# Rotary scores over 128 rows with each head's rotary k standing twice, in a float32 hybrid encoder trunk

## The chip, the cores and the metric

The kernel runs on one core of one Trainium2 chip. Its engines, as the profile names them: PE (TensorE, matmuls) with PEld (its weight loads), DVE (VectorE), ACT (ScalarE), POOL (GpSimd) and SP (SyncE), whose queue issues nearly all DMAs. The metric is the device time of one execution in microseconds, as a median over runs.

## The reference

A trunk of two layers on 512 positions and 2048 channels, in float32. The first layer is a gated pooling mixer; from its output come one shared key and value side, and then a layer of latent attention with 16 heads:

```python
def qk_norm_rope(t, g, cos, sin):
    t = rmsnorm(t, g)
    return jnp.concatenate([t[..., :QK_NOPE], apply_rope(t[..., QK_NOPE:], cos, sin)], axis=-1)
...
def pool_mixer_layer(x, norm_g, w_in, w_group, scale, w_out):
    h = rmsnorm(x, norm_g)
    proj = h @ w_in
    u, gate = proj[..., :W_A], proj[..., W_A:]
    u = u.reshape(B, S, N_POOL_GROUPS, G_A)
    pooled = jnp.stack(
        [causal_mean_pool(u[:, :, gi], w) - u[:, :, gi] for gi, w in enumerate(POOL_WINDOWS)],
        axis=2)
    y = jnp.einsum('bsgc,gcd->bsgd', pooled, w_group).reshape(B, S, W_A) * scale
    y = y * jax.nn.silu(gate)
    return x + y @ w_out
...
    for i in range(S // QBLOCK):
        q0, k_end = i * QBLOCK, (i + 1) * QBLOCK
        s = jnp.einsum('bqhd,bkhd->bhqk', q[:, q0:k_end], k[:, :k_end],
                       preferred_element_type=jnp.float32) * scale
        s = jnp.where(mask[None, None], s, -1e30)
        p = jax.nn.softmax(s, axis=-1).astype(v.dtype)
        outs.append(jnp.einsum('bhqk,bkhd->bqhd', p, v[:, :k_end]))
```

The pool windows are 2, 4, 8 and 16, one for each group of channels. The mask is causal by chunks of 64 positions. Each head's q and k have 128 plain channels (`QK_NOPE`) and 64 rotary ones (`QK_ROPE`), so a score is a sum over 192 products. The rotary k is the same for all heads up to the norm, which is taken per head.

## The kernel before

Products of float32 are made of three matmuls: each operand is split into a high part (a cast to fp32r, on ScalarE) and a low part (the rest, a subtraction on VectorE); high by high, low by high and high by low are added in PSUM. `split` (L144, L145) does it for activations and `load_w` (L120 to L122) for weights, which are loaded through the SP queue into `raw`.

**Stages, with their times in the profiled execution.** The pool mixer's input product runs to 698.6 us, within `with ExitStack() as c1`, where it has tile pools of its own (`xcp`, `epool`, `w7`, `ps7`); its results go to DRAM tiles (`scr`, L337). Then come the grouped products (`pooled_tile` and `y_tile`, weights `awg`) and the mixer's output product (`awo`) to about 1240. `pooled_tile` loads a 128x512 piece of the mixer's input from DRAM (L391) into a tile of `tpool` and pools and splits it; `y_tile` loads the gate (L400) and multiplies by `awg`. Eight pieces of group 0 are made ahead of the first product. `tpool` has six buffers of 512 columns (tag "t", tiles called `tt_`) and is opened once, for the whole kernel. Latent products and gates follow to about 1530, attention to 1835, and the output product (`bwo`) to the end.

**Attention** goes by head pairs, `hg` from 0 to 7. What a pair needs is prepared by `prep_units`: the kv product in four pieces (`kv_unit`, k0 to k3 in the planner's list, L570 to L572), the q product in four (`q_unit`, q0 to q3, L590 to L592, its result copied from PSUM by ScalarE, L595), the norms, and six transposes of 128x512 (`tr_unit`, L655): T0 and T1 turn the plain k of the two heads, T2 the rotary k of both heads at once (head 0 in rows 0 to 63, head 1 in rows 64 to 127), T3 and T4 the plain q and T5 the rotary q, again of both heads. `attn_units` has for each head four score units of 128 queries by 128, 256, 384 and 512 keys (`score_unit`, L696), each followed by the softmax (memset of the masked corner L697, reduction L699, its scaling L701, exponential L704 on ScalarE, reciprocal L705, scaling L706), the transposes of its probabilities (`pt_unit`, L715) and, after every second, the product with the values (`pv_unit`, L740 to L742).

The order in which the units are written comes from a hand-made list (`PREP`) and two constants that say when a piece of the next pair's preparation comes due among the units of this pair's attention. From there on the order on each engine is set by a scheduler in the tile framework: each engine then runs its own list strictly in order, and waits on semaphores for the others. A wait is for a whole tile, not for the rows of it that are used, and an engine that reads a PSUM tile is ordered behind another engine that reads it. PSUM tiles: three `mm` (products), two `sc` (scores), two `tr` (transposes), one `ov`.

**Rotary parts before.** T2 leaves one tile `kh` with the high parts of both heads (one cast of 128x512, L659) and per head a tile that has its low part in its own 64 rows (L660, L661) and a copy of its high part in the other 64 (L662, L663). T5 leaves per head a tile with the high part of q in the head's own 64 rows (L668, L669) and the low part in the others (L670, L671). A score unit is five matmuls: three of the plain parts over 128 rows, then high by high over the head's 64 rows, then one over 128 rows which adds high q by low k and low q by high k.

Of the kernel before, what the change touches and what calls it, by code (L numbers as in the profile page):

```python
# [14 lines left out]
P = 128  # L15
S = 512
# [35 lines left out]
def trunk_kernel(  # L52
# [21 lines left out]
    spool = ctx.enter_context(tc.tile_pool(name="spool", bufs=4))  # L74
    tpool = ctx.enter_context(tc.tile_pool(name="tpool", bufs=6))
    dpool = ctx.enter_context(tc.tile_pool(name="dpool", bufs=16, space=bass.MemoryType.DRAM))

    def xt(shape=(P, S), dt=F32):
        return xpool.tile(list(shape), dt, tag="x", name="xt")
# [7 lines left out]
    def tt_(n=S, dt=F32):  # L87
        return tpool.tile([P, n], dt, tag="t", name="tt_")

# [9 lines left out]
    def f(ap):  # L99
        return ap.bitcast(F32)  # L100
# [154 lines left out]

    with ExitStack() as c1:
        xcp = c1.enter_context(tc.tile_pool(name="xcp", bufs=NJ))
        epool = c1.enter_context(tc.tile_pool(name="epool", bufs=2))
# [123 lines left out]
    bpool = ctx.enter_context(tc.tile_pool(name="bpool", bufs=32, **tile_))  # L382
    xpool = ctx.enter_context(tc.tile_pool(name="xpool", bufs=16, **tile_))
    ps = ctx.enter_context(tc.tile_pool(name="ps", bufs=2, space=bass.MemoryType.PSUM, **tile_))

# [39 lines left out]


    xkv, xb, spill = [], [], []
    accs = [tt_(), tt_()]
# [80 lines left out]
    for t in range(4):  # L509
        junk = spool.tile([P, 192], F32, tag="junk", name="junk", bufs=2)  # L510
        A.activation(junk[:, 0:64], kr[:, t, :], AF.Square, accum_out=kr2[:, t:t + 1])
# [51 lines left out]
    def kv_unit(hg, t):  # L563
# [12 lines left out]
        for h in range(2):  # L576
            junk = spool.tile([P, 192], F32, tag="junk", name="junk", bufs=2)
            A.activation(junk[:, 0:128], d["kraw"][a][:, b, h * P:(h + 1) * P], AF.Square,
                         accum_out=d["ssk"][:, 2 * t + h:2 * t + h + 1])

    def q_unit(hg, t):
# [14 lines left out]
        for h in range(2):  # L596
            junk = spool.tile([P, 192], F32, tag="junk", name="junk", bufs=2)
            A.activation(junk, q[:, h, :], AF.Square, accum_out=d["ssq"][:, 2 * t + h:2 * t + h + 1])
# [43 lines left out]
    def tr_unit(hg, u):  # L642
# [13 lines left out]
        if u == 2:  # L656

            kh, k0, k1 = xt(dt=F32R), bt(), bt()
            A.copy(kh, p)  # L659
            V.tensor_tensor(k0[0:64, :], p[0:64, :], f(kh[0:64, :]), ALU.subtract)  # L660
            V.tensor_tensor(k1[64:128, :], p[64:128, :], f(kh[64:128, :]), ALU.subtract)  # L661
            V.tensor_copy(k0[64:128, :], f(kh[0:64, :]))  # L662
            V.tensor_copy(k1[0:64, :], f(kh[64:128, :]))  # L663
            d["kr"] = (kh, k0, k1)
            return
        if u == 5:
            q0, q1 = bt(), bt()
            A.copy(q0[0:64, :], p[0:64, :])  # L668
            A.copy(q1[64:128, :], p[64:128, :])  # L669
            V.tensor_tensor(q0[64:128, :], p[0:64, :], f(q0[0:64, :]), ALU.subtract)  # L670
            V.tensor_tensor(q1[0:64, :], p[64:128, :], f(q1[64:128, :]), ALU.subtract)  # L671
            d["qr"] = (q0, q1)
            return
# [9 lines left out]
    def score_unit(hg, h, i):  # L683
# [220 lines left out]
```

## Time and profile before

| | us |
|---|---|
| median of 3 runs | 1993.39 |
| lowest and highest | 1992.2, 1994.09 |
| the profiled execution | 1993.23 |
| its span in the trace | 1991.4 |
| its stages: pool mixer input | 0 to 698.6 |
| grouped and output products | to about 1240 |
| latent products, gates | to about 1530 |
| attention | to about 1835 |
| output product | to 1991.4 |

A row of the profile has the line of the kernel, the engine, the operation, what it writes and reads by the program's names, the shapes and the count; then the busy time in us and the mean of one in ns; then the idle time of the engine just before, with what ended it. In timelines a row starts with the start and the duration in us, and a bracket at its end is idle time before it. PE overlaps consecutive matmuls, so the time that one takes of the engine is read from the distance of starts. The granted clock of PE is given as a share of full speed.

### The profile page before, as it was taken

How to read it: one execution, taken by the hardware profiler on the slowest of the kernel's cores; microseconds unless marked ns; L12 is line 12 of the kernel's file. 1: busy time of each engine (PE TensorE's matmuls, PEld its weight loads, DVE VectorE, ACT ScalarE, POOL GpSimd, SP SyncE). 2: the span in 40 equal slices, each digit the busy share in tenths (PEclk: the TensorE clock that was granted, in tenths of full speed). 3: DMA queues.
4: the chain of work that ended last, by engine and by line, in shares of the span. 5: the costliest groups of instructions: out<-in, count | busy, mean ns of one | idle time of the engine just before them, and what ended most of it. 6: DMA issues, size and time to landing. Idle time of an engine off the chain costs nothing.

```text
span 1991.4 us, 30647 instructions
## 1 busy us (share of the span) xinstructions
PE 1941.2 (97%) x11372; PEld 1717.5 (86%) x11372; DVE 1289.7 (65%) x2291; ACT 815.8 (41%) x1527; POOL 299.1 (15%) x434
## 2 busy tenths in 40 slices
PE   5699999999999999999999999999999999999999
PEld 5699999999999978888888888888888788878887
DVE  6778866666666589377496567473344878787422
ACT  5433333333333353233333354233244767675221
POOL 2733432222222200000000000000010211110000
PEclk9799999999999999999999999999999999999999
DMA  4534544444444374344344344323332111121632
GB/s 157 175 111 134 168 129 138 128 135 125 135 127 134 121 243 159 106 127 148 112 128 136 107 144 132 94 92 99 96 94 76 51 42 46 50 65 48 211 121 87
DMA packets 167110, 235.53 MB, mean 118 GB/s; under 512 B 14640, under 2 KB 93360, under 8 KB 166960
## 3 DMA queue, kind: packets, MB, share of 16 engines
q1 hardware_dynamic: 166672, 233.37, 37.6%
q8 instruction: 89, 1.46, 0.3%
q14 instruction: 61, 0.50, 0.1%
q10 hardware_dynamic: 288, 0.20, 0.0%
HBM read 208.35 MB, written 25.17 MB: 117 GB/s over the span
## 4 chain that ended last, share of the span: by engine, by line
PE 93%; DVE 3%; DMA 1%; ACT 1%; issue 1%; POOL 0%; SPq 0%; DVEq 0%; ACTq 0%; POOLq 0%
PE mm L141 16%; PE mm L139 16%; PE mm L140 16%; PE k L320 10%; PE k L316 10%; PE k L318 10%; PE sc L696 3%; PE mm L570 1%; PE mm L571 1%; PE mm L572 1%; DMA raw<-awin 1%; PE tr L655 1%; PE mm L592 1%; PE mm L590 1%; PE mm L591 1%; PE tr L715 1%
## 5 line engine op out<-in xcount | busy, mean ns | idle before, releaser
L316 PE MATMUL k<-xh,hi 128*128 128x256 f32 x1792 | 493.7, 287 | 31.3 <-ACT hi L299 31.1
L318 PE MATMUL k<-xl,hi 128*128 128x256 f32 x1792 | 495.7, 286 | 0.9 <-DVE xl L284 0.8
L121 ACT CAST whi<-raw 128x512 fp32r<-128x512 f32 (+2 forms) x421 | 256.1, 611 | 537.0 <-PE mm L140 461.6
L320 PE MATMUL k<-xh,lo 128*128 128x256 f32 x1792 | 450.3, 287 | 4.9 <-DVE lo L300 4.9
L122 DVE TENSOR_TENSOR wlo<-raw,whi 128x512 fp32r<-128x512 f32 (+2 forms) x421 | 282.1, 672 | 225.6 <-ACT whi L121 221.8
L299 ACT CAST hi<-raw 128x1792 fp32r<-128x1792 f32 x128 | 216.2, 1690 | 406.9 <-PE k L320 260.5
L300 DVE TENSOR_TENSOR lo<-raw,hi 128x1792 fp32r<-128x1792 f32 x128 | 266.2, 2080 | 179.2 <-ACT hi L299 179.2
L316 PEld LDWEIGHTS k<-xh,hi 128*128 128x128 f32 x1792 | 348.0, 195 | 32.3 <-ACT hi L299 31.9
L318 PEld LDWEIGHTS k<-xl,hi 128*128 128x128 f32 x1792 | 349.5, 195 | 1.3 <-DVE xl L284 1.3
L141 PE MATMUL mm<-bt,wlo 128*128 128x512 f32 x860 | 335.5, 390 | 0.0
L139 PE MATMUL mm<-bt,whi 128*128 128x512 f32 x860 | 334.7, 389 | 0.0
L140 PE MATMUL mm<-bt,whi 128*128 128x512 f32 x860 | 334.5, 389 | 0.0
L320 PEld LDWEIGHTS k<-xh,lo 128*128 128x128 f32 x1792 | 321.6, 195 | 6.9 <-DVE lo L300 6.4
L139 PE MATMUL mm<-at,whi 128*128 128x512 f32 x516 | 202.1, 393 | 2.6 <-ACT whi L121 2.5
L141 PE MATMUL mm<-at,wlo 128*128 128x512 f32 x516 | 202.3, 392 | 1.7 <-DVE wlo L122 1.7
L140 PE MATMUL mm<-at,whi 128*128 128x512 f32 x516 | 202.3, 392 | 0.0
L141 PEld LDWEIGHTS mm<-bt,wlo 128*128 128x128 f32 x860 | 161.5, 188 | 34.2 <-issue 0.5
L139 PEld LDWEIGHTS mm<-bt,whi 128*128 128x128 f32 x860 | 161.5, 188 | 33.7 <-issue 0.2
L140 PEld LDWEIGHTS mm<-bt,whi 128*128 128x128 f32 x860 | 161.5, 188 | 33.5
L295 POOL TENSOR_TENSOR raw<-raw 128x256 f32<-128x256 f32 x128 | 107.0, 836 | 421.8 <-DVE raw L293 408.1
L141 PEld LDWEIGHTS mm<-at,wlo 128*128 128x128 f32 x516 | 97.4, 189 | 23.8 <-DVE wlo L122 3.6
L139 PEld LDWEIGHTS mm<-at,whi 128*128 128x128 f32 x516 | 97.5, 189 | 23.0 <-ACT whi L121 3.0
(1148 smaller groups left out, 2434.3 us busy)
## 6 DMA issues: line engine op xcount, KB each, us to landing
raw<-awin SPq DMA_DIRECT2D x256, 256.0 KB, 3.3
raw<-awo SPq DMA_DIRECT2D x128, 256.0 KB, 2.7
raw<-bwin SPq DMA_DIRECT2D x80, 256.0 KB, 2.8
raw<-awg SPq DMA_DIRECT2D x64, 256.0 KB, 2.9
raw<-bwo SPq DMA_DIRECT2D x59, 256.0 KB, 2.8
scr<-e SPq DMA_DIRECT2D x56, 256.0 KB, 2.6
raw<-wkvb SPq DMA_DIRECT2D x32, 256.0 KB, 3.1
raw<-wqb SPq DMA_DIRECT2D x32, 192.0 KB, 2.4
```

The source lines that it names most:

```text
L121: A.copy(hi[:, :n], raw[:, :n])
L122: V.tensor_tensor(lo[:, :n], raw[:, :n], f(hi[:, :n]), ALU.subtract)
L139: T.matmul(dst, wh, xh, start=first, stop=False)
L140: T.matmul(dst, wh, xl, start=False, stop=False)
L141: T.matmul(dst, wl, xh, start=False, stop=last)
L295: G.tensor_tensor(c[:, :, 6, :], c[:, :, 4, :], c[:, :, 2, :], ALU.add)
L299: A.copy(hi, c[:, :, 1:8, :])
L300: V.tensor_tensor(lo, c[:, :, 1:8, :], f(hi), ALU.subtract)
L316: T.matmul(dst, hi[:, j % 2, wi, :], xh[j][:, xi, :], start=first, stop=False, skip_group_check=True)
L318: T.matmul(dst, hi[:, j % 2, wi, :], xl[j][:, xi, :], start=False, stop=False, skip_group_check=True)
L320: T.matmul(dst, lo[:, j % 2, wi, :], xh[j][:, xi, :], start=False, stop=last, skip_group_check=True)
L696: T.matmul(s[:, 0:n], l, r, start=(j == 0), stop=(j == 4))
```

## The change

**Scores.** The fourth matmul goes over 128 rows instead of 64. For that a head's rotary k stands twice: `krh` has its high part in rows 0 to 63 and again in 64 to 127, `krl` likewise its low part. The rotary q tile has high over low, for both heads now in the same rows (high in 0 to 63). The fourth matmul adds high q by high k and low q by high k, the fifth high q by low k and also low q by low k, a product that was not made before.

**The tiles from T2 and T5.** Of T2, per head and half, there is a cast and then a subtraction, eight steps where there were five; the two halves of a head are in the same tiles. Of T5 the same four steps are written in another order: cast, subtraction, cast, subtraction.

**Pools.** Head 0's `krh` is a tile of `rpool`. `junk`, a scratch output of ScalarE's sums of squares, has one buffer instead of two. `tpool` becomes three pools in turn: one that lives during the pool mixer's input product, one (opened behind `xpool`) for the grouped and output products, one for the rest. The second's six tiles take addresses that `w7`, the weight tiles of the pool mixer, had; before, `tpool` overlapped nothing.

```diff
--- before.py
+++ after.py
...
-    tpool = ctx.enter_context(tc.tile_pool(name="tpool", bufs=6))
+    ca = ExitStack()
+    tp = [None]
...
     def tt_(n=S, dt=F32):
-        return tpool.tile([P, n], dt, tag="t", name="tt_")
+        return tp[0].tile([P, n], dt, tag="t", name="tt_")
...
     with ExitStack() as c1:
+        tp[0] = c1.enter_context(tc.tile_pool(name="tpool1", bufs=6))
         xcp = c1.enter_context(tc.tile_pool(name="xcp", bufs=NJ))
...
     xpool = ctx.enter_context(tc.tile_pool(name="xpool", bufs=16, **tile_))
+    tp[0] = ca.enter_context(tc.tile_pool(name="tpool2", bufs=6, **tile_))
...
+    ca.close()
+    tp[0] = ctx.enter_context(tc.tile_pool(name="tpool3", bufs=6, **tile_))
     xkv, xb, spill = [], [], []
...
-        junk = spool.tile([P, 192], F32, tag="junk", name="junk", bufs=2)
+        junk = spool.tile([P, 192], F32, tag="junk", name="junk", bufs=1)
...
         if u == 2:
 
-            kh, k0, k1 = xt(dt=F32R), bt(), bt()
-            A.copy(kh, p)
-            V.tensor_tensor(k0[0:64, :], p[0:64, :], f(kh[0:64, :]), ALU.subtract)
-            V.tensor_tensor(k1[64:128, :], p[64:128, :], f(kh[64:128, :]), ALU.subtract)
-            V.tensor_copy(k0[64:128, :], f(kh[0:64, :]))
-            V.tensor_copy(k1[0:64, :], f(kh[64:128, :]))
-            d["kr"] = (kh, k0, k1)
+
+            d["kr"] = []
+            for h in range(2):
+                src = p[h * 64:h * 64 + 64, :]
+                kh, kl = (xt(dt=F32R) if h else rpool.tile([P, S], F32R, tag="r", name="kr0")), bt()
+                for o in (0, 64):
+                    A.copy(kh[o:o + 64, :], src)
+                    V.tensor_tensor(kl[o:o + 64, :], src, f(kh[o:o + 64, :]), ALU.subtract)
+                d["kr"].append((kh, kl))
             return
         if u == 5:
             q0, q1 = bt(), bt()
-            A.copy(q0[0:64, :], p[0:64, :])
-            A.copy(q1[64:128, :], p[64:128, :])
-            V.tensor_tensor(q0[64:128, :], p[0:64, :], f(q0[0:64, :]), ALU.subtract)
-            V.tensor_tensor(q1[0:64, :], p[64:128, :], f(q1[64:128, :]), ALU.subtract)
+            for h, q in enumerate((q0, q1)):
+                src = p[h * 64:h * 64 + 64, :]
+                A.copy(q[0:64, :], src)
+                V.tensor_tensor(q[64:128, :], src, f(q[0:64, :]), ALU.subtract)
             d["qr"] = (q0, q1)
...
-        krh, krx = d["kr"][0], d["kr"][1 + h]
+        krh, krl = d["kr"][h]
         qh, ql_ = d[("T", 3 + h)]
         qr = d["qr"][h]
         qs = slice(i * P, (i + 1) * P)
-        hs = slice(h * 64, h * 64 + 64)
         ops = [(qh[:, qs], kh[:, 0:n]), (qh[:, qs], kl[:, 0:n]), (ql_[:, qs], kh[:, 0:n]),
-               (qr[hs, qs], krh[hs, 0:n]), (qr[:, qs], krx[:, 0:n])]
+               (qr[:, qs], krh[:, 0:n]), (qr[:, qs], krl[:, 0:n])]
```

How this moves instructions is seen in the order on three engines. Lines of the kernel after are a few higher (L655 becomes L660, L696 L702, L715 L721, L391 L394, L595 L600, L704 L710). First TensorE around the rotary and plain q transposes of a steady head pair, before: the transposes of T5 (`tt__15837` is the rotary q), two score units of this pair's second head, T3 between them, the transposed probabilities of an earlier unit, T4, and the first score unit of the next pair.

```order
L655 MATMUL tr<-cs,tt__15837 128x128 x4
L696 MATMUL sc<-bt 128x384 x3
L696 MATMUL sc<-xt,bt 128x384
L696 MATMUL sc<-bt 128x384
L655 MATMUL tr<-cs,xt 128x128 x4
L696 MATMUL sc<-bt 128x512 x3
L696 MATMUL sc<-xt,bt 128x512
L696 MATMUL sc<-bt 128x512
L715 MATMUL tr<-cs,tt__16006 128x128 x4
L655 MATMUL tr<-cs,xt 128x128 x4
L696 MATMUL sc<-bt 128x128 x3
L696 MATMUL sc<-xt,bt 128x128
```

The same place after (`tt__15857` is the rotary q):

```order
L660 MATMUL tr<-cs,tt__15857 128x128 x4
L702 MATMUL sc<-bt 128x512
L702 MATMUL sc<-xt,bt 128x512
L702 MATMUL sc<-bt 128x512
L660 MATMUL tr<-cs,xt 128x128 x4
L702 MATMUL sc<-bt 128x128 x2
L721 MATMUL tr<-cs,tt__16030 128x128 x4
L702 MATMUL sc<-bt 128x256 x2
L660 MATMUL tr<-cs,xt 128x128 x4
L702 MATMUL sc<-bt 128x128
L702 MATMUL sc<-kr_15964,bt 128x128
L702 MATMUL sc<-bt 128x128
```

T5 stood ahead of the unit of 384 columns and now stands within the one of 512; T3, which stood ahead of that one, is now behind it, directly ahead of the next pair's first scores; and the next pair's units of 128 and 256 are begun in turn, two matmuls each, with T4 in between.

ScalarE around the rotary k, before: the cast of T2 (L659), then the two copies of the q product, a weight cast and an exponential.

```order
L121 CAST whi<-raw 128x512
L144 CAST xt<-tr 128x128
L659 CAST xt<-tr 128x512
L595 COPY xt<-mm 128x384 x2
L121 CAST whi<-raw 128x512
L704 ACTIVATE tt__15934,sm<-sc,nm,qy 128x384
L598 ACTIVATE junk,ssq<-xt 128x192 x2
```

The same place after, one pair on (`kr_16534` is head 0's high part, the casts on `xt` at L669 are head 1's):

```order
L710 ACTIVATE tt__16524,sm<-sc,nm,qy 128x384
L669 CAST kr_16534<-tr 64x512
L145 CAST xt<-tr 128x2x128
L710 ACTIVATE tt__16600,sm<-sc,nm,qy 128x512
L669 CAST kr_16534<-tr 64x512
L669 CAST xt<-tr 64x512
L600 COPY xt<-mm 128x384 x2
L710 ACTIVATE tt__16661,sm<-sc,nm,qy 128x128
L145 CAST bt<-tr 128x512
L710 ACTIVATE tt__16732,sm<-sc,nm,qy 128x256
L603 ACTIVATE junk,ssq<-xt 128x192
L669 CAST xt<-tr 64x512
```

The four casts are spread over this stretch, with the copies of the q product behind the third and the fourth eleven rows behind the first.

SP's queue at the end of the pool mixer's input product, before: its last stores to DRAM, three loads of `awg` and the seventh and eighth loads of pooled input (the first six, `tt__7476` to `tt__7506`, stand much earlier, among the loads of the mixer's last weights):

```order
L290 DMA raw<-awin 128x2x256 x6
L337 DMA scr<-e 256x1x256
L337 DMA scr<-e 128x512
L120 DMA raw<-awg 128x512 x3
L417 DMA xt<-xT 128x512
L391 DMA tt__7512<-scr 128x512
L417 DMA xt<-xT 128x512
L391 DMA tt__7518<-scr 128x512
```

And after, where the first load of pooled input (`tt__7480`) is the one that waits for the last matmul on the weight tiles that lay there:

```order
L339 DMA scr<-e 256x1x256
L339 DMA scr<-e 128x512
L394 DMA tt__7480<-scr 128x512
L394 DMA tt__7486<-scr 128x512
L394 DMA tt__7492<-scr 128x512
L394 DMA tt__7498<-scr 128x512
L394 DMA tt__7504<-scr 128x512
L394 DMA tt__7510<-scr 128x512
L121 DMA raw<-awg 128x512
L339 DMA scr<-e 256x1x256
L339 DMA scr<-e 128x512
L394 DMA tt__7516<-scr 128x512
```

All six first loads of pooled input now stand here, ahead of the first load of `awg`.

More of the change, by code (lines that the diff above doesn't have):

```diff
@@ L576, in kv_unit @@
         for h in range(2):
-            junk = spool.tile([P, 192], F32, tag="junk", name="junk", bufs=2)
+            junk = spool.tile([P, 192], F32, tag="junk", name="junk", bufs=1)
             A.activation(junk[:, 0:128], d["kraw"][a][:, b, h * P:(h + 1) * P], AF.Square,
@@ L596, in q_unit @@
         for h in range(2):
-            junk = spool.tile([P, 192], F32, tag="junk", name="junk", bufs=2)
+            junk = spool.tile([P, 192], F32, tag="junk", name="junk", bufs=1)
             A.activation(junk, q[:, h, :], AF.Square, accum_out=d["ssq"][:, 2 * t + h:2 * t + h + 1])
```

## Prediction

> **What bounds the kernel now.** I read the page first, then the windows of the attention stage, then the waits of TensorE there. The page's shares of busy time, and the first line of its chain:
>
> ```profile
> PE 1941.2 (97%) x11372; PEld 1717.5 (86%) x11372; DVE 1289.7 (65%) x2291; ACT 815.8 (41%) x1527; POOL 299.1 (15%) x434
> ...
> PE 93%; DVE 3%; DMA 1%; ACT 1%; issue 1%; POOL 0%; SPq 0%; DVEq 0%; ACTq 0%; POOLq 0%
> ```
>
> TensorE is busy 97% of the span and 93% of the chain, so matmul time taken away is time gained, unless something else then ends last. The change touches attention, so what counts is the limit there. Two windows, columns busy us of PE, PEld, DVE, ACT, POOL, then granted clock; the first is one steady head pair, the second the last pair, whose attention has no preparation beside it:
>
> ```profile
> 1584.31:1623.45 39.14, 38.51 (x218) 32.37 (x217) 31.99 (x114) 27.55 (x96) 6.61 (x16) 1.00 0.16 48
> ...
> 1779.90:1835.00 55.10, 54.17 (x280) 42.86 (x281) 42.56 (x139) 32.29 (x88) 3.66 (x9) 1.00 0.18 54
> ```
>
> A head pair takes 39.14 us and TensorE idles 0.63 of it. VectorE is busy 31.99, 82%: the second limit is near. TensorE's waits over five such pairs (total, times, longest):
>
> ```profile
> PE tr L715 <- DVE bt L671: 1.8, 5, 0.4
> PE tr L655 <- DVE bt L678: 1.3, 5, 0.3
> ```
>
> 3.1 us over five pairs, 0.62 each, both at the transposes around the q tiles. All the rest of VectorE's and ScalarE's work is hidden now.
>
> **The matmuls.** What the 64-row matmul costs is read from starts, since matmuls overlap. TensorE and its weight loads in two adjacent score units (384 and 512 columns), with the matmuls of 384 and 512 columns that ran back to back nearby:
>
> ```profile
> 1622.24 0.33 PE L590 MATMUL mm<-whi,at 128*128 128x384 f32 x1
> ...
> 1623.11 0.34 PE L592 MATMUL mm<-wlo,at 128*128 128x384 f32 x1
> 1623.29 0.68 PE L696 MATMUL sc<-bt 128*128 128x384 f32 x3
> 1623.89 0.44 PE L696 MATMUL sc<-xt,bt 64*128 64x384 f32 x1
> 1624.26 1.14 PE L696 MATMUL sc<-bt 128*128 128x384 f32 x4
> 1625.33 0.50 PE L696 MATMUL sc<-xt,bt 64*128 64x512 f32 x1
> 1625.76 0.51 PE L696 MATMUL sc<-bt 128*128 128x512 f32 x1
> 1626.11 0.27 PE L715 MATMUL tr<-cs,tt__15866 128*128 128x128 f32 x1
> ```
>
> ```profile
> 1623.89 0.18 PEld L696 LDWEIGHTS sc<-xt,bt 64*128 64x128 f32 x1 [0.25 <-issue]
> 1624.26 0.71 PEld L696 LDWEIGHTS sc<-bt 128*128 128x128 f32 x4 [0.18 <-issue]
> 1625.33 0.18 PEld L696 LDWEIGHTS sc<-xt,bt 64*128 64x128 f32 x1 [0.36 <-issue]
> ```
>
> ```profile
> 1629.42 0.40 PE L572 MATMUL mm<-wlo,at 128*128 128x512 f32 x1
> ...
> 1630.58 0.39 PE L571 MATMUL mm<-whi,at 128*128 128x512 f32 x1
> ```
>
> From 1622.24 to 1623.11 five matmuls of 384 columns start, 0.174 us apart; from 1629.42 to 1630.58 five of 512, 0.232 apart. Ten score matmuls at that pace take 5×0.174 + 5×0.232 = 2.03 us. They take 1626.11 − 1623.29 = 2.82, so 0.79 too long, 0.39 per unit. The loads show where: the weight load into 64 rows, and the 128-row one behind it, are not begun ahead under the running matmul but wait 0.18 to 0.36 us, with nothing to wait for by the profile. All 64 units have one such matmul (16 of each width):
>
> ```profile
> L696 PE MATMUL sc<-xt,bt 64*128 64x512 f32 x16 | 8.0, 499 | 0.0
> ```
>
> The new matmul is 128-row, with as many columns: an ordinary fifth of the unit. The gain on TensorE is 64 × 0.39 = 25.0 us, 8 × 0.39 = 3.1 per pair; I bound it by 22 and 27 (0.35 and 0.42 a unit), since the two narrower widths are taken to be like these.
>
> The Trainium skill, TensorEngine Tiling (Array Packing), section Overview, Theoretical Speedup, says that a contraction of at most 64 rows can go up to twice as fast with the array split, which speaks against this change: at half of a mean 0.145 us, giving up 64 such matmuls would cost about 5 us (an estimate by that page). The rows disagree (0.43 us from the start at 1625.33 to the next, where 128 rows take 0.232); its Key Properties say that a change of tiling mode drains TensorE, which the held loads fit.
>
> **The new tiles.** Durations of the pieces, from the groups by form and from the timelines of VectorE and ScalarE in one such pair (start, duration):
>
> ```profile
> L595 ACT COPY xt<-mm 128x384 f32<-128x384 f32 x32 | 14.3, 480 | 3.9 <-PE mm L592 3.9
> ...
> L678 DVE SCALAR_TENSOR_TENSOR bt<-tr,gqk,bt 128x512 fp32r<-128x512 f32 x15 | 10.8, 722 | 3.3 <-ACT bt L677 3.0
> ...
> L677 ACT ACTIVATE bt<-tr,gqk 128x512 fp32r<-128x512 f32 x15 | 10.3, 688 | 8.0 <-PE tr L655 8.0
> ...
> L671 DVE TENSOR_TENSOR bt<-tr,bt 64x512 fp32r<-64x512 f32 x8 | 5.5, 694 | 0.1
> ...
> L668 ACT CAST bt<-tr 64x512 fp32r<-64x512 f32 x8 | 4.6, 580 | 2.9 <-PE tr L655 2.8
> ```
>
> ```profile
> 1605.83 0.37 ACT L144 CAST xt<-tr 128x256 fp32r<-128x256 f32 x1
> 1606.10 0.79 ACT L704 ACTIVATE tt__15712<-sc,nm,qy 128x512 f32<-128x512 f32 x1
> ```
>
> ```profile
> 1604.47 0.67 DVE L699 TENSOR_REDUCE nm<-sc 128x1 f32<-128x512 f32 x1
> ...
> 1605.38 0.42 DVE L145 TENSOR_TENSOR xt<-tr,xt 128x256 fp32r<-128x256 f32 x1
> ...
> 1605.87 0.11 DVE L697 MEMSET sc<- 64x64 f32 x1
> ...
> 1606.50 0.28 DVE L699 TENSOR_REDUCE nm<-sc 128x1 f32<-128x128 f32 x1
> ...
> 1607.10 0.15 DVE L705 RECIPROCAL sm<-sm 128x1 f32<-128x1 f32 x1
> ...
> 1607.57 0.48 DVE L706 TENSOR_SCALAR tt__15712<-tt__15712,sm 128x512 f32<-128x512 f32 x1
> ```
>
> Busy time grows little: four 64-row casts for one cast (ScalarE +2.3 us a pair at most, 4 × 0.58), and two more subtractions in place of two copies (VectorE +1.4 at most, 2 × 0.69). VectorE's 31.99 + 1.4 = 33.4 would still fit a period of 39.1 − 3.1 = 36.0. What matters is order: in the built program each of the eight steps of the k tile waits for the one before it, across engines, and of the q tile the second cast now waits for the first subtraction. What stands behind a waiting cast on ScalarE waits as well. I walk both places with these durations and no time for handoffs.
>
> K tile, from the end of its transposes (0). ScalarE: cast 0.58, cast of the transposed probabilities 0.95, exponential of 512 columns 1.74 (its sum 0.09 later, an estimate), second k cast 2.41. VectorE: subtraction 1.27, memset 1.38, subtraction of the probabilities 1.80, reciprocal behind the exponential 1.98, reduction 2.26, scaling 2.74, second k subtraction 3.43. ScalarE: third k cast 4.01, and only then the copy of the q projection, 4.49, which frees the PSUM buffer of the next kv product. TensorE's own work is put at 0.058 us for 128 columns (a quarter of 0.232) and 0.09 for a transpose (an estimate: nearer to that than to the 0.27 of one alone). It has 0.67 us to do, then waits for the probabilities' cast until 0.95 (0.28), works to 1.07, waits for the exponential to free a score buffer until 1.74 (0.67), works 1.36 to 3.10, and waits for that buffer until 4.49 (1.39). Sum 2.3 us.
>
> Q tiles, from the end of the 512-column unit into which the rotary q transposes now fall (0). VectorE: memset 0.11, first q subtraction 0.80, reduction 1.47, 1.62, second q subtraction 2.31. ScalarE: second cast, behind the first subtraction, 1.38, and behind it the scaled cast of the next transposes, 2.07. TensorE has only those transposes (0.36), then waits until 2.07 for the next pair's first scores: 1.71. The rest follows alike: 0.1 each before two transposes and before the value products, then 1.4 before a transpose whose buffer VectorE frees behind two reductions (0.28 and some 0.4) and another scaled subtraction (0.72). Sum 3.4 us.
>
> Together 5.7 a pair, of which 0.6 is there already: 5.1 new against 3.1 gained. Five steady pairs: 25.5. The pair whose preparation comes first and is laid out differently: half, 2.6. For the last pair's 55 us the window shows VectorE free for 12.5 us, so its gain stays. Bounds of these waits: 5 us in all (the next engine is early nearly everywhere, as now) and 38 (a third more, since handoffs were left out). I take 28, near the walk's end, because it follows the program's own waits.
>
> **The pools.** The tiles of pooled input move to a place that overlaps the pool mixer's weight tiles, and so the first of their loads now waits for the last matmul of that stage; five more, and then the first weights of the next stage, stand behind it in SP's queue. Now three of those weight loads are issued before the last matmul. TensorE at the first matmuls of the next stage, the rate of all DMAs from 698 to 722 us in 40 slices with the time from issue to landing of a first one, and the window behind (granted clock third from the end):
>
> ```profile
> 701.16 0.80 PE L139 MATMUL mm<-at,whi 128*128 128x512 f32 x1 [2.54 <-ACT whi L121]
> ...
> 703.14 0.80 PE L141 MATMUL mm<-at,wlo 128*128 128x512 f32 x1 [0.76 <-DVE wlo L122]
> ```
>
> ```profile
> GB/s 0 0 0 0 0 20 259 389 379 239 236 311 379 270 232 273 338 314 376 396 403 396 403 413 403 410 393 393 382 399 382 386 389 389 382 382 386 389 386 386
> ...
> tt__7512<-scr SPq DMA_DIRECT2D x1, 256.0 KB, 2.7
> ```
>
> ```profile
> 701.10:707.90 6.80, 5.98 (x14) 4.30 (x15) 6.80 (x13) 3.74 (x8) 0.00 (x0) 0.53 0.88 278
> ```
>
> TensorE ends the pool mixer at 701.16 − 2.54 = 698.6. The first load, issued then, lands 2.7 later; the six others follow 0.67 us apart (256 KB at the 390 GB/s of the full queue), so the weights land at 705.3, and with a cast of 0.6 (the 0.58 above) the first matmul starts at 705.9, for 701.16: +4.8, less some of the 0.76, which data that lie there by then can spare. I take +4.5, with bounds of 2 (all of that and part of the later work's slack) and 7 (another stall of 2 on weights that queue behind). Half clock is paid now and would be paid then.
>
> The other edit, one junk buffer for two, costs nothing: all its writes are ScalarE's own, in order.
>
> **The sum.** −25.0 + 28 + 4.5 = +7.5. The profiled execution took 1993.23, span 1991.4, against a median of 1993.39 (1992.2 to 1994.09), so the two agree: 1993.4 + 7.5 = 2001. By the bounds of the waits alone it is 1993.4 − 25.0 + 4.5 + 5 = 1978 to 2011.
>
> **Rivals.** *The gain stays.* If the chains overlap with later slack, the pair falls by most of its 3.1 us. For it: VectorE idles 7 us a pair. Against it: TensorE's place in the queue is fixed, and slack elsewhere doesn't feed a wait here. With 5 us of waits 1978, with half of the walked 28, 1987; it decides below 20.5 us of waits, 3.7 a pair. *They cancel*, at waits of 16.5 to 24.5: 1989.4 to 1997.4, within 4 us of no change. *The clock drops.* The idle of 2.54 us at the handover is followed by a granted clock of 0.53 over 6.8 us. If waits of 1.4 to 1.7 did the same, two a pair would cost 2 × 6.8 × 0.47 = 6.4 us each of six pairs, 38 in all: 2039. Against it, this wait of 1.06 and the clock after it:
>
> ```profile
> 1544.97 0.79 PE L696 MATMUL sc<-xt 128*128 128x384 f32 x3 [1.06 <-ACT tt__14734 L704]
> ```
>
> ```profile
> 1543.80:1550.60 6.80, 5.74 (x26) 4.03 (x26) 5.17 (x15) 6.12 (x18) 1.53 (x5) 1.00 0.33 89
> ```
>
> The Trainium skill, TensorE: Matmul & The Clock Gate, section What's actually happening, puts half clock behind an idle window of about 3.4 us, longer than any wait here; by it this rival falls, though the 2.54 above was shorter and did bring 0.53. *The change does not do what it says*: the held loads come from changing operands and stay; then nothing offsets the 32.5, and it ends at 2026.
>
> **Chances.** Waits about as walked 0.44 (1998 to 2010); cancel 0.16; gain stays, half or nearly whole, 0.34; clock 0.03; held loads stay 0.03. 0.2%, 4 us, is what a measurement of this kernel can tell from none. Faster 0.34, same 0.16, slower 0.50. The range runs from 1975 to 2013: the 1978 and 2011 of the waits, each moved by about half of what the bounds of the other two terms add (27 and 2 instead of 25.0 and 4.5 one way, 22 and 7 the other). The likeliest case alone has 1998 to 2010.
>
> **What would show it.** Right: score units of about 1.2 us at 512 columns and no held loads; TensorE waiting 1 us and more for the q projection's copy and for the scaled cast, in each pair, at clock 1.00; a pair of 41 us; a first matmul of the second stage at 706. Wrong: a pair below 38 us, these waits under half a microsecond, or VectorE above 95% of a pair, which would make it a bound that the walk left out.

## The result, and the profile after

The change takes 2016.34 us (median of 4 runs, 2015.03 to 2017.9) against 1993.03 before: a ratio of 1.0117, 95% interval 1.0099 to 1.0134. Slower was forecast, but the 23 us lie outside the range, which ended at 2013. The page of after, as that of before was shown:

```profile
span 2016.1 us, 30664 instructions
...
PE 1933.3 (96%) x11372; PEld 1718.0 (85%) x11372; DVE 1309.6 (65%) x2291; ACT 829.6 (41%) x1551; POOL 297.7 (15%) x434
...
PE 85%; DVE 6%; ACT 4%; DMA 3%; issue 1%; POOL 0%; SPq 0%; DVEq 0%; ACTq 0%; POOLq 0%
```

TensorE is busy 8 us less, in a span 25 us longer: of the chain that ended last it held 93% and holds 85%, and VectorE, ScalarE and DMAs got the rest. So time went into waits. To see where, I set the n-th matmul of after against the n-th of before (both have 11372):

| from | to | before | after | more |
|---|---|---|---|---|
| first matmul | last of the pool mixer's input product | 683.0 | 683.3 | +0.3 |
| there | matmul 5600 (some 220 on) | 57.3 | 70.7 | +13.4 |
| there | first transpose of T2 | 717.4 | 717.2 | -0.1 |
| there (attention) | 500 matmuls from the end | 401.1 | 413.1 | +12.0 |
| there | last matmul | 113.1 | 113.1 | 0.0 |

The sum is 25.6, and the first matmul is 0.9 earlier. Two places, then: the handover behind the pool mixer, and attention. TensorE at the handover in after:

```profile
697.68 0.28 PE L322 MATMUL k<-xh,lo 128*128 128x256 f32 x1
707.14 0.79 PE L140 MATMUL mm<-at,whi 128*128 128x512 f32 x1 [9.17 <-ACT whi L122]
...
723.18 0.52 PE L140 MATMUL mm<-at,whi 128*128 128x512 f32 x1 [2.01 <-ACT whi L122]
```

```profile
PE mm L140 <- ACT whi L122: 11.2, 2, 9.2
PE mm L142 <- DVE wlo L123: 1.8, 1, 1.8
```

The first wait is 9.17 us for 2.54, and there are two more, of 2.0 and 1.8, where before had one of 0.76. SP's queue in the same stretch shows what the weights stand behind:

```profile
697.99 0.34 SPq L394 DMA_DIRECT2D tt__7480<-scr  x1
698.38 0.43 SPq L394 DMA_DIRECT2D tt__7486<-scr  x1
...
700.28 0.43 SPq L394 DMA_DIRECT2D tt__7510<-scr  x1
700.75 0.43 SPq L121 DMA_DIRECT2D raw<-awg  x1
```

Six loads go ahead of the first weights, issued at 700.75, 14 us later than before. The windows (busy us of PE, PEld, DVE, ACT, POOL, then clock, DMA share, GB/s) show half clock behind the long wait, and again behind the later ones:

```profile
707.14:713.30 6.16, 6.16 (x15) 4.76 (x16) 3.93 (x7) 3.99 (x6) 0.00 (x0) 0.50 1.05 397
...
720.00:728.00 8.00, 5.99 (x20) 4.16 (x19) 3.34 (x5) 2.31 (x5) 0.00 (x0) 0.79 1.05 387
728.00:736.00 8.00, 6.21 (x27) 4.57 (x26) 5.08 (x15) 3.26 (x6) 0.00 (x0) 1.00 0.31 110
736.00:745.00 9.00, 9.00 (x33) 7.25 (x34) 6.97 (x24) 3.15 (x7) 0.11 (x1) 0.81 0.59 176
```

9.7 us of the 13.4 are idle (9.17 + 2.01 + 1.8 less 2.54 + 0.76); the drops behind the two later waits cost 8.00 × 0.21 + 9.00 × 0.19 = 3.4 us more, which before hadn't.

In attention, the same pair of score units as was shown of before (384 and 512 columns):

```profile
1681.69 0.77 PE L702 MATMUL sc<-bt 128*128 128x384 f32 x3
1682.30 0.34 PE L702 MATMUL sc<-kr,bt 128*128 128x384 f32 x1
1682.47 1.03 PE L702 MATMUL sc<-bt 128*128 128x384 f32 x4
1683.34 0.39 PE L702 MATMUL sc<-kr,bt 128*128 128x512 f32 x1
1683.57 0.40 PE L702 MATMUL sc<-bt 128*128 128x512 f32 x1
1683.80 0.27 PE L721 MATMUL tr<-cs,tt__16456 128*128 128x128 f32 x1
```

Ten matmuls in 2.11 us for 2.82: the held loads are gone. TensorE's waits over two steady head pairs (total, times, longest; the last row is one pair's exponential, the other pair's wait is alike):

```profile
PE sc L702 <- ACT bt L684: 2.9, 2, 1.4
PE mm L575 <- ACT xt L600: 1.5, 2, 0.8
PE tr L660 <- DVE sc L703: 0.8, 2, 0.4
PE ov L747 <- DVE xt L146: 0.7, 2, 0.3
PE sc L702 <- ACT tt__16600 L710: 0.4, 1, 0.4
```

The two largest are those of the walk: the next pair's first scores wait 1.44 us for the scaled cast of the late plain q, and the kv product 0.76 for the q projection's copy. How the first comes about is read from three engines. TensorE first:

```profile
1702.88 0.46 PE L702 MATMUL sc<-bt 128*128 128x128 f32 x2 [1.44 <-ACT bt L684]
```

ScalarE, whose second rotary q cast waits for VectorE, with the scaled cast behind it:

```profile
1701.53 0.58 ACT L677 CAST bt<-tr 64x512 fp32r<-64x512 f32 x1 [1.21 <-DVE bt L678]
1702.14 0.69 ACT L684 ACTIVATE bt<-tr,gqk 128x512 fp32r<-128x512 f32 x1
```

And VectorE:

```profile
1700.81 0.68 DVE L678 TENSOR_TENSOR bt<-tr,bt 64x512 fp32r<-64x512 f32 x1
```

The subtraction ends at 1701.49, the cast starts at 1701.53, the scaled cast at 1702.14, the scores at 1702.88. This wait stands in four pairs in turn; the two steady pairs ahead of them have waits of 0.68 and 1.29 before plain q transposes instead. The clock behind it does not always fall. Windows at its end in the four pairs:

```profile
1661.00:1664.00 3.00, 1.60 (x13) 1.49 (x14) 2.83 (x8) 2.41 (x5) 0.00 (x0) 1.00 0.00 0
1703.00:1706.00 3.00, 3.00 (x16) 2.92 (x16) 1.87 (x5) 1.27 (x4) 0.00 (x0) 0.53 0.00 0
1743.50:1746.50 3.00, 1.78 (x15) 1.68 (x15) 2.87 (x7) 2.27 (x5) 0.00 (x0) 1.00 0.03 5
1785.50:1788.50 3.00, 3.00 (x16) 3.00 (x16) 1.57 (x4) 1.20 (x4) 0.00 (x0) 0.50 0.00 0
```

In two of four it is at half, for 3.41 us each time, which costs 1.7 us each. From T2 to T2 the four pairs take 40.4, 41.9, 40.4 and (the last, with other work in it) 47.7 us; the two ahead of them have 41.4 and 41.9 without a fall, so the length of a pair alone doesn't show one.

Why in these two? The trace's record of the granted clock changes only at points of a fixed grid. In this execution the falls from 700 us on begin at 703.05, 723.53, 737.19, 1703.16 and 1785.08, which lie whole multiples of 3.413 us apart, and each lasts 3.41 us or a whole multiple of it. Here is the stretch of this grid in which each of the four waits lies (or begins), with TensorE's busy time first:

```profile
1658.79:1662.20 3.41, 1.83 (x12) 1.14 (x10) 2.90 (x9) 2.24 (x6) 0.00 (x0) 1.00 0.00 0
1699.75:1703.16 3.41, 1.57 (x9) 0.90 (x7) 3.15 (x8) 2.18 (x5) 0.00 (x0) 1.00 0.01 2
1740.71:1744.12 3.41, 2.22 (x13) 1.40 (x12) 2.90 (x11) 2.24 (x7) 0.00 (x0) 1.00 0.03 7
1781.67:1785.08 3.41, 1.63 (x11) 0.94 (x9) 2.90 (x9) 2.24 (x7) 0.00 (x0) 1.00 0.02 5
```

The second and the fourth wait, which end at 1702.88 and 1785.05, lie wholly in one stretch. TensorE is busy for less than half of it (1.57 and 1.63 of 3.41 us), and the next stretch is at half clock. The first and the third, which end at 1662.40 and 1744.72, are cut by an edge of the grid, TensorE is busy for more than half (1.83 and 2.22), and the clock stays. I counted the same over the traces of all twelve kernels, from 690 us on, in stretches at full clock: 31 had TensorE busy for 49% or less, and all 31 were followed by half clock; of 4461 with 50% or more three were, with 67, 69 and 73%.

What TensorE's time in attention is made of, per group of matmuls: each matmul from its start to the next start, less idle time before the next. `b_zero` is an experiment below; the last column counts the waits of 0.03 us or more, and the score tiles hold some matmuls of the gates and the output product too, the same in all three.

| kernel | score tiles | kv and gates (512) | transposes | values | q (384) | idle | waits |
|---|---|---|---|---|---|---|---|
| before | 99.4 | 162.9 | 35.4 | 34.9 | 62.4 | 6.0 | 15 |
| after | 81.1 | 167.0 | 39.3 | 35.9 | 62.2 | 27.7 | 59 |
| b_zero | 76.8 | 163.7 | 34.7 | 34.9 | 62.3 | 10.8 | 23 |

Idle grew by 21.7 us. The scores gained 18.3 instead of the 22.6 that `b_zero` has by its 128 rows, and the same transposes, kv products and values take 9.0 more, though nothing about them changed. Against `b_zero`, `after` has 4.3 us more in the score tiles and 8.8 in the rest. Where these 13.1 lie is seen when the median distance of each shape in `b_zero` is taken as its pace: the matmuls directly ahead of a wait hold 5.2 us more than in `b_zero`, those directly behind one 4.4, and all others 3.4, about what the two drops of the clock cost. So 9.6 us go with the 36 more waits, 0.27 each: next to a wait a matmul has no neighbour to overlap with.

### The profile page after: what moved, and what is told of

It reads as the page before. It is cut to its first block, busy times and chain, and to the rows that moved or that the text cites. A ratio compares the mean times of both kernels' runs of the same rounds, so it can differ in the third digit from the quotient of the medians.

```text
span 2016.1 us, 30664 instructions
## 1 busy us (share of the span) xinstructions
PE 1933.3 (96%) x11372; PEld 1718.0 (85%) x11372; DVE 1309.6 (65%) x2291; ACT 829.6 (41%) x1551; POOL 297.7 (15%) x434
## 4 chain that ended last, share of the span: by engine, by line
PE 85%; DVE 6%; ACT 4%; DMA 3%; issue 1%; POOL 0%; SPq 0%; DVEq 0%; ACTq 0%; POOLq 0%
PE mm L140 16%; PE mm L142 16%; PE mm L141 15%; PE k L322 10%; PE k L318 10%; PE k L320 10%; DMA raw<-awin 1%; PE mm L575 1%; PE sc L702 1%; PE mm L576 1%; PE mm L577 1%; DVE lo L302 1%; PE tr L721 1%; DMA raw<-wkvb 1%; PE mm L595 1%
## 5 line engine op out<-in xcount | busy, mean ns | idle before, releaser
L297 POOL TENSOR_TENSOR raw<-raw 128x256 f32<-128x256 f32 x128 | 103.6, 810 | 417.9 <-DVE raw L295 401.1
L140 PEld LDWEIGHTS mm<-at,whi 128*128 128x128 f32 x516 | 98.2, 191 | 33.8 <-ACT whi L122 13.4
```

What stands on the lines that cost most here:

```text
L140: T.matmul(dst, wh, xh, start=first, stop=False)
L297: G.tensor_tensor(c[:, :, 6, :], c[:, :, 4, :], c[:, :, 2, :], ALU.add)
```

## The experiments

Ten kernels. The pools first: the kernel before with the change's pools alone.

```diff
-    tpool = ctx.enter_context(tc.tile_pool(name="tpool", bufs=6))
+    ca = ExitStack()
+    tp = [None]
...
+        tp[0] = c1.enter_context(tc.tile_pool(name="tpool1", bufs=6))
...
+    tp[0] = ca.enter_context(tc.tile_pool(name="tpool2", bufs=6, **tile_))
...
+    ca.close()
+    tp[0] = ctx.enter_context(tc.tile_pool(name="tpool3", bufs=6, **tile_))
```

> The kernel before with the pools of the change alone: tpool split in three. Theory A (the two traces differ by 13.4 us between the last matmul of the pool mixer's input product and the stretch behind the next 100 matmuls, and this is the pools alone): 1993 + 13.4 = 2006.4 us, with a first wait of about 9 us and two later ones of about 2. Rival B (only the first delay of 4.5 us that I worked out is the pools', the rest comes from elsewhere): 1997 to 1999.

It took 2004.96 us, ratio 1.0058 (1.0043 to 1.0073), and its waits at the handover are those of after:

```profile
PE mm L140 <- ACT whi L122: 11.1, 2, 9.1
PE mm L142 <- DVE wlo L123: 1.8, 1, 1.8
```

From the last pool matmul to matmul 5600 it has 70.5 us, as after has. The pools alone make this loss: 11 us in the times, 13 in the traces. The other way round, the kernel after with the one pool of before:

```diff
+    tpool = ctx.enter_context(tc.tile_pool(name="tpool", bufs=6))
...
-        tp[0] = c1.enter_context(tc.tile_pool(name="tpool1", bufs=6))
...
-    tp[0] = ca.enter_context(tc.tile_pool(name="tpool2", bufs=6, **tile_))
...
-    ca.close()
-    tp[0] = ctx.enter_context(tc.tile_pool(name="tpool3", bufs=6, **tile_))
```

> The kernel after with the pools of before (one tpool for the whole kernel); scores, casts and junk as after. Theory A: 2016.3 - 13.4 = 2003 us, since what attention loses (37 us of new waits and half clock against 25 gained, +12) is independent of the pools. Rival B: 2010 to 2012, if the pools account for 4.5 only.

2005.56, ratio 1.0058 (1.0041 to 1.0075): 11 us back, near theory A, and clear of B. The split was not needed for space: this kernel has all of the change but the split. Is it the weights behind the waiting loads? The three pools again, but the waiting loads on another queue:

```diff
-        nc.sync.dma_start(x, raws[g * 8 + o])
+        (nc.sync if g else nc.gpsimd).dma_start(x, raws[g * 8 + o])
```

> The kernel before with the three pools, and the eight first loads of pooled input issued by GpSimd's queue instead of SP's, so that they still wait for the last matmul but no weights stand behind them. Theory A (the cost of the pools is the weights behind the waiting loads in SP's queue, then the stalls and the half clock that follow): 1994 + 2 to 5, and a first wait of 4 to 5 us. Rival B (the late pooled input itself sets the start, eight pieces of it): 2003 to 2006 as with SP's queue.

1998.11, ratio 1.0023 (1.0013 to 1.0032). Its waits at the handover:

```profile
PE mm L140 <- ACT at L145: 4.5, 1, 4.5
PE mm L140 <- ACT whi L122: 3.8, 2, 1.9
```

The first wait is halved, and it is now for the cast of pooled input (`at`), no longer for weights; to matmul 5600 it is 63.3 us. So of 13 us some 7 were the weights behind the loads in SP's queue, and the other 6 lie at the late input and at two later stalls on weights.

Now the matmul alone: the kernel before, with the fourth matmul over all rows.

```diff
-               (qr[hs, qs], krh[hs, 0:n]), (qr[:, qs], krx[:, 0:n])]
+               (qr[:, qs], krh[:, 0:n]), (qr[:, qs], krx[:, 0:n])]
```

> The kernel before with one edit: the fourth score matmul goes over all 128 rows of the tiles as they are, so it adds products of q's low part with the other head's rotary k, and its scores are not the reference's. No tile, pool or cast changes. Theory A (a 64-row matmul costs 0.39 us too much in each of 64 units, whatever stands around it): 1993 - 25 = 1968 us, up to 1973 if the faster TensorE then waits for VectorE here and there. Rival B (the held weight loads come with the change of operands and stay): 1990 to 1996.

1975.21, ratio 0.9908 (0.9893 to 0.9923): 19 us faster. A steady pair takes 36.9 us for 39.1. Rival B is out. The gain is smaller than A's 25 for two reasons. On TensorE it is 22.9, not 25.0 (and 22.6 in `b_zero` below): by widths of 128, 256, 384 and 512 columns the 16 units of each save 4.3, 6.1, 6.1 and 6.4 us, so the narrowest 0.27 each and the others 0.38 to 0.40. And idle grew by 4.5, more than half of it at the transposes of probabilities behind the rotary q, where before had 2.2 over the same six pairs:

```profile
PE tr L714 <- DVE bt L671: 4.6, 6, 0.8
```

This kernel has the order of before on TensorE throughout. What of the rest is order, and what the work of the new tiles? The kernel after with the pools of before, and all casts ahead of all subtractions, in T2 and in T5:

```diff
-                for o in (0, 64):
-                    A.copy(kh[o:o + 64, :], src)
-                    V.tensor_tensor(kl[o:o + 64, :], src, f(kh[o:o + 64, :]), ALU.subtract)
+            for o in (0, 64):
+                for h in range(2):
+                    A.copy(d["kr"][h][0][o:o + 64, :], p[h * 64:h * 64 + 64, :])
+            for o in (0, 64):
+                for h in range(2):
+                    kh, kl = d["kr"][h]
+                    V.tensor_tensor(kl[o:o + 64, :], p[h * 64:h * 64 + 64, :], f(kh[o:o + 64, :]), ALU.subtract)
...
-            for h, q in enumerate((q0, q1)):
-                src = p[h * 64:h * 64 + 64, :]
-                A.copy(q[0:64, :], src)
-                V.tensor_tensor(q[64:128, :], src, f(q[0:64, :]), ALU.subtract)
+            A.copy(q0[0:64, :], p[0:64, :])
+            A.copy(q1[0:64, :], p[64:128, :])
+            V.tensor_tensor(q0[64:128, :], p[0:64, :], f(q0[0:64, :]), ALU.subtract)
+            V.tensor_tensor(q1[64:128, :], p[64:128, :], f(q1[0:64, :]), ALU.subtract)
```

> The kernel after with the pools of before, and in T2 and T5 all casts written ahead of all subtractions; the same eight and four steps of the same shapes, the same scores. In its order on TensorE the plain q transposes stand ahead of the 384- and 512-column units again, as in the kernel before. Theory A (what costs is the late place of the q transposes, which the alternating casts and subtractions bring about): near the 1975 of the kernel with the matmul alone, 1975 to 1983. Rival B (what costs is the added work on ScalarE and VectorE, three casts and two subtractions for two copies): 1995 to 2005, as with the alternating order.

1992.4, ratio 0.9993 (0.9983 to 1.0002): no change against before, 13 us better than with the alternating order, and between the two theories, nearer to B's. In its order T3 stands ahead of both units, one unit earlier than in before, and other places differ from before too. A steady pair takes 38.95 us. ScalarE and TensorE in it:

```profile
1624.68 0.58 ACT L665 CAST kr<-tr 64x512 fp32r<-64x512 f32 x1 [0.28 <-PE tr L655]
...
1626.46 0.58 ACT L665 CAST xt<-tr 64x512 fp32r<-64x512 f32 x1
1627.06 0.86 ACT L595 COPY xt<-mm 128x384 f32<-128x384 f32 x2
```

```profile
1627.59 0.50 PE L570 MATMUL mm<-whi,at 128*128 128x512 f32 x1 [1.12 <-ACT xt L595]
```

The wait for the scaled cast is gone with the order. The wait for the q projection's copy is left, and longer (1.12 for 0.76): the copy stands behind all four casts. With either grouping alone:

```diff
-            for h, q in enumerate((q0, q1)):
-                src = p[h * 64:h * 64 + 64, :]
-                A.copy(q[0:64, :], src)
-                V.tensor_tensor(q[64:128, :], src, f(q[0:64, :]), ALU.subtract)
+            A.copy(q0[0:64, :], p[0:64, :])
+            A.copy(q1[0:64, :], p[64:128, :])
+            V.tensor_tensor(q0[64:128, :], p[0:64, :], f(q0[0:64, :]), ALU.subtract)
+            V.tensor_tensor(q1[64:128, :], p[64:128, :], f(q1[0:64, :]), ALU.subtract)
```

This is the edit of `a_t5` (T5 grouped, T2 alternating); `a_t2` has the other half of the diff of `a_group`.

> As the last, but only T2 grouped: T5 keeps cast, subtraction, cast, subtraction. Its order on TensorE still has the first plain q transposes directly ahead of the next pair's first scores. Theory A (the late q transposes cost): 1990 to 2005, little better than with both alternating. Rival C (the eight alternating steps of the rotary k cost, by ScalarE's queue behind them): 1976 to 1985.

> The kernel after with the pools of before and T5 grouped (both casts, then both subtractions); T2 keeps its eight alternating steps. With a_oldpool (both alternating, 2005.6), a_t2 (T2 grouped, 2005.9) and a_group (both, 1992.4) this fills a table of two by two. In its order the plain q transposes still stand directly ahead of the next pair's scores. Theory A (the order decides, and either alternation is enough to bring the late one about): 2000 to 2006. Rival C (the alternation in T5 alone was the loss of 13 us): 1990 to 1995.

`a_t2` took 2005.88, ratio 1.0057 (1.004 to 1.0073), `a_t5` 2011.3, ratio 1.009 (1.0075 to 1.0105); with both alternating it was 2005.6, with both grouped 1992.4. So neither alternation is the loss by itself: as long as either stands, TensorE's order has the plain q late, and at least these 13 us are lost. Theory A's ranges are missed by little for `a_t2` (2006) and by 5 us for `a_t5` (2011); rival C is out for both. `a_t5` is worse than both alternating by half clock: its clock stands at half for 20.5 us in attention, that of `a_oldpool` for 10.2, and half of that is lost.

But the late plain q is not what TensorE waits for in all of them. In `a_t2` its scaled cast costs little, and the copy of the q projection, behind four casts in a row, costs most:

```profile
PE mm L570 <- ACT xt L595: 9.2, 6, 1.7
...
PE sc L700 <- ACT bt L682: 1.7, 5, 0.3
```

The late place and the alternation come together in these three kernels, so what the late place costs by itself is not shown by them.

The tile could be made with fewer steps. Each head's scaled rotary k is written twice, side by side, before it is transposed; then T2 is four transposes, one cast and one subtraction of 128x512 for each head (T5 grouped, pools of before):

```diff
-        d["krs"] = tt_()
+        d["krs"] = [tt_(), tt_()]
...
-                A.activation(d["krs"][:, c * 64:(c + 1) * 64], krr[:, t, :], AF.Copy, scale=y[:, c:c + 1])
+                A.activation(d["krs"][h][:, t * P:(t + 1) * P].rearrange("p (a d) -> p a d", a=2),
+                             krr[:, t:t + 1, :].broadcast_to([P, 2, 64]), AF.Copy, scale=y[:, c:c + 1])
...
+            for h in range(2):
+                p = tr()
+                for t in range(4):
+                    T.transpose(p[:, t * P:(t + 1) * P], d["krs"][h][:, t * P:(t + 1) * P], ident)
+                kh, kl = (xt(dt=F32R) if h else rpool.tile([P, S], F32R, tag="r", name="kr0")), bt()
+                split(p, kh, kl)
```

> The kernel after with the pools of before, and the doubled rotary k made another way: ScalarE writes each head's scaled rotary k twice side by side before the transposes, T2 is four transposes per head (eight in all), and then one cast and one subtraction of 128x512 per head; T5 has its two casts ahead of its two subtractions. The scores are those of the kernel after. Theory A (the loss in attention comes from chains of casts and subtractions that wait for each other in turn): most of the 25 us stays, less 2.9 us for 32 more transposes and some 5 to 10 us of waits: 1976 to 1982. Rival B (the loss comes from where the transposes stand in TensorE's order, whatever the casts): 1990 to 2003.

1998.06, ratio 1.0022 (1.0013 to 1.0031): in rival B's range. Its largest wait in attention:

```profile
PE sc L694 <- ACT bt L676: 8.7, 6, 1.5
```

It has four long steps for the k tile, no alternation, and still the late plain q. So I moved that by the list of the preparation alone:

```diff
-PREP = "B k0 k1 k2 k3 K q0 q1 T0 T2 q2 T1 q3 T5 T3 T4 S".split()
+PREP = "B k0 k1 k2 k3 K q0 q1 T2 T0 q2 q3 T3 T5 T1 T4 S".split()
```

> The kernel with the doubled rotary k made before its transposes (1998 us), with one edit: in the list of the preparation the plain q of the first head is transposed (T3) ahead of the rotary q and T1, so that in TensorE's order T3 no longer stands directly ahead of the next pair's first scores. Theory A (the late T3 is what cost, 8.7 us of waits for its scaled cast, with restarts and half clock behind them): 1976 to 1986. Rival B (the extra transposes, the wider scalings of the rotary k and one more buffer of tpool cost it): 1994 to 2000.

1993.32, ratio 1.0002 (0.9992 to 1.0011). The 8.7 us of waits are gone, but only 5 us with them: others took their place.

```profile
PE ov L739 <- DVE xt L145: 3.6, 5, 0.7
PE tr L664 <- DVE bt L145: 1.8, 6, 0.3
PE mm L570 <- DVE bt L145: 1.2, 1, 1.2
```

Idle fell from 20.4 to 16.5 us. The transposes take 44.3 us in attention, against 34.7 in `b_zero`: some 10 us for 32 more, what they hold beside waits among it. So most of the cost of this way of making the tile stayed, as rival B had it (0.7 us below its range), and theory A held only for a part.

Last, a 128-row matmul with as little new work as I could find. The high k of a head gets a tile of its own, its other half set to zero by GpSimd; the rest is as before.

```diff
-            kh, k0, k1 = xt(dt=F32R), bt(), bt()
-            A.copy(kh, p)
+            z0, z1, k0, k1 = rpool.tile([P, S], F32R, tag="r", name="kr0"), xt(dt=F32R), bt(), bt()
+            G.memset(f(z0[64:128, :]), 0.0)
+            G.memset(f(z1[0:64, :]), 0.0)
+            A.copy(z0[0:64, :], p[0:64, :])
+            A.copy(z1[64:128, :], p[64:128, :])
...
-               (qr[hs, qs], krh[hs, 0:n]), (qr[:, qs], krx[:, 0:n])]
+               (qr[:, qs], krh[:, 0:n]), (qr[:, qs], krx[:, 0:n])]
```

> The kernel before with a 128-row fourth matmul made right another way: each head's high rotary k has a tile of its own whose other 64 rows GpSimd sets to zero, so two casts of 64 rows stand for the one of 128; subtractions and copies as before, pools as before. Theory A (the gain is the matmul's and keeps if the order stays): 1975 to 1979. Rival B (the waits for GpSimd's two memsets, or the added cast, hold the chain of the rotary k): 1985 or more.

1975.07, ratio 0.9907 (0.9893 to 0.9922): the fastest, 18 us below before, 41 below after. ScalarE around its rotary k, and the two score units that were shown of before and after:

```profile
1621.97 0.58 ACT L661 CAST kr<-tr 64x512 fp32r<-64x512 f32 x1
1622.57 0.58 ACT L662 CAST xt<-tr 64x512 fp32r<-64x512 f32 x1
1623.18 0.86 ACT L595 COPY xt<-mm 128x384 f32<-128x384 f32 x2
```

```profile
1619.19 0.68 PE L698 MATMUL sc<-bt 128*128 128x384 f32 x3
...
1621.22 0.27 PE L717 MATMUL tr<-cs,tt__15878 128*128 128x128 f32 x1
```

Two casts ahead of the copy, no wait for it at the kv product, TensorE's order around the q transposes as before, and ten matmuls in 2.03 us, which is the pace of two undisturbed units.

## Why the prediction was wrong

**The matmuls: right, a little too large.** 25.0 us was the forecast, 22 to 27 its bounds; TensorE's own gain is 22.6 in `b_zero` and 22.9 in `b_mm128`. The term took the 384- and 512-column units for all widths; the 128-column unit saves 0.24 to 0.27 us, not 0.39. That the loads are held because of the 64 rows, and not because operands change, `b_mm128` shows.

**The waits in attention: the places were right in four pairs of six, their cost was mis-sized.** The walk gave 28 us. Measured against 22.6 gained, attention lost 12.0 + 22.6 = 34.6, within its bound of 38 and for partly other reasons. Idle time alone is 21.7, less than the walk's: of the waits that it named, the scaled cast's has 1.44 us (walked 1.71), the q copy's 0.76 (1.39), the exponential's 0.38 (0.67), and the one before a transpose, walked at 1.4, some 0.4. But the walk priced a wait at its idle time. With it go some 10 us at the matmuls next to the waits, and 3.4 of half clock. That the total stayed within the bound is luck in part: idle time was taken too high, and these 13 us were put at nothing. Order and added work both have a share: from `b_mm128` (the matmul alone) to `a_oldpool` (all but the pools) 30 us are lost; grouping the same steps brought 13 of them back, and 17 stayed.

**The rival of the clock: partly true, and priced in the wrong way.** I had it at 0.03 and as all or nothing. The clock fell behind 1.44 us of wait in two of four pairs, for 1.7 us each. The argument against it was one wait of 1.06 without a fall, and the price was that of the handover, 6.8 us at half clock. The Trainium skill, TensorE: Matmul & The Clock Gate, section What's actually happening, puts the fall behind an idle window of about 3.4 us; here a wait of 1.44 us sufficed, and the same wait one pair on did not. The same section calls the window free-running, by which it would depend on where in it the wait lies. The trace agrees: the falls stand on a grid of 3.413 us, and the two came where the wait lay wholly within one stretch of it. But no stretch was idle throughout: 46 and 48% busy sufficed.

**The pools: this step failed.** "I take +4.5, with bounds of 2 (all of that and part of the later work's slack) and 7 (another stall of 2 on weights that queue behind)". Measured 13.4 in the trace, 11 in the times. The first start was placed 1.2 too early: 705.9 for 707.14, though the stage before ended 0.7 earlier, so the wait itself was 1.9 longer than worked out. What the sum left out is behind it: two stalls of 1.8 and 2.0, of which the bound held one, and half clock behind both. "Half clock is paid now and would be paid then" holds for the first start only. With 13.4 in place of 4.5 the sum is 2010, and the range, moved by as much, holds the 2016. The matmuls and the waits together missed as much, 9.0 us (+3.0 forecast, +12.0 measured), but each of them lies within its own bounds; the pools' term alone does not.

**What stays open.** Why alternating casts and subtractions make the scheduler place the q transposes later is open; shown is that they do. What the late place costs by itself was tried only with the k tile made otherwise, where moving T3 (and T0, T1 and T2 with it) brought 5 us. Between `a_group` (1992.4) and `b_zero` (1975.1) lie 17 us, for two more casts and two subtractions instead of two copies, the order that goes with them, and one `junk` buffer for two, which no run tested by itself. By the traces, 9.4 of the 17 are idle time and 7.2 are at the matmuls next to waits; the wait for the q copy, 6.5 us at the kv product, is the largest that `b_zero` doesn't have. Why three falls of the clock came behind stretches that were 67 to 73% busy is open too.

## What to carry to other kernels

A matmul that is cheaper on the bound engine pays only as far as the tiles that it needs come as early as before: look first for a form that leaves the steps and the order of the other engines alone (zeros in the unused rows did, doubled rows did not). Price a wait on TensorE at more than its idle time (here 0.27 us more each). And where a pool is moved, ask who had its addresses last, and what is queued behind the first load that must wait for that.

## What the runs showed of the hardware

A 64-row matmul among 128-row ones cost 0.38 to 0.41 us more than a 128-row one at 256 to 512 columns, and 0.24 to 0.27 at 128. The granted clock fell to 0.5 behind waits of 1.44 and 2.01 us, for 3.41 us each time; behind 9.17 us it stayed there for 6 us from the first matmul. In these traces it fell at points 3.413 us apart or multiples of that, and what went with a fall was less the length of a wait than TensorE's busy share in the stretch of 3.41 us ahead: 49% or less in 31 stretches, with 31 falls; 50% or more in 4461, with three. Waits of 1.12 us in every pair (`a_group`) left the steady pairs at 38.95 us each, without a fall among them. And 36 more waits went with 9.6 us more between the starts of the matmuls next to them, beside the idle time itself.
